# Other filler quotas in the attention stage, and GpSimd's long operations in pieces of 256 columns

## The chip, the cores and the metric

The kernel runs on one NeuronCore of a Trainium2 chip. The metric is the device time of one execution in microseconds (us), smaller is better. The engines are named as in the profile: PE is TensorE (matrix products and transposes), PEld its loads of weights, DVE is VectorE, ACT is ScalarE, POOL is GpSimd, SP is SyncE, which starts most of the transfers. Each engine works off its own instructions in a fixed order, and an instruction waits until what it needs from other engines is there.

## The reference, cut to what matters

One layer of a decoder for 1024 tokens of 1024 numbers. A normalized input goes through one projection into four token mixers (pooling, a short gated convolution, a Conformer convolution, differential attention with 4 heads), each 256 wide; their outputs go through one output projection and are added to the input; then comes a gated feed-forward part with 2816 inner columns.

```python
h = rms_norm(x, norm1_g)
z = h @ w_in                                   # 1024 x 2304, split into the mixers' inputs
# attention: two score maps per head, causal, with a bias per distance
p = softmax(sc, axis=-1);  a = p[:, :, 0] - lam * p[:, :, 1];  o = rms_norm(a @ v) * (1 - lam_init)
mix = concatenate([y_pool, y_sconv, y_conf, y_attn], axis=-1)
x = x + mix @ w_out
h2 = rms_norm(x, norm2_g)
x = x + (silu(h2 @ w_gate) * (h2 @ w_up)) @ w_down
```

All tensors are float32.

## The kernel before

**Products in three parts.** For TensorE each float32 matrix is split into a rounded part, hi, and the rest, lo = value - hi, and a product is the sum of three: hi times hi, hi times lo, lo times hi (`mm3`, L137 to L140; `mms`, L603 to L606, for the output projection). For a weight `wsplit` does this (L124 to L135): a transfer into the staging tile st, a cast to whi on the engine that a table names, and on GpSimd the subtraction to wlo, 128 x 1024, at L134.

**The attention stage** (some 220 to 450 us of the span). The tokens stand in four groups p of 256, and a unit is one p with one of four heads h: 16 units. For each half i of the group and each of the two score maps m, a unit makes scores on TensorE (sc, L673), VectorE adds the bias and takes the minimum (L680, L681), ScalarE makes the exponentials pt (L684), VectorE combines the two maps with a factor cf (L686 to L688). Then TensorE transposes pt (tp, L699), ScalarE and VectorE split it into at (L703, L704), and TensorE multiplies with the values (av, L708). After a second head the result oT is transposed (L720); after the fourth, VectorE normalizes the group. Ahead of the units the normalized queries qn are split and transposed (`stack_T`, L498 to L513): ScalarE makes the rounded part, GpSimd or VectorE the rest in kst (L506), TensorE transposes (L510). The two halves of a kst pair share one buffer: the second half can be written only when the transposes of the first are done.

**Fillers.** While a unit's chain runs, TensorE does other work in between: `gen_partial` (L608 to L635) is the output projection of the three other mixers in 16 items of 18 matmuls, 288 in all (tile fm, here called projections). For each item the mixer's tile is split into sp (lo on GpSimd, L627), the six weight tiles come from `load_wo`, and at the end ScalarE copies the sum and GpSimd adds the residual (x, L633, 14 of 16 items; the other two on VectorE). Later fillers are `out_attn` (L743 to L774, the attention's part of the output projection, its addition at L772), the second norm with its transposes (L190), and the first gate and up products of the feed-forward part (gu items). How many fillers follow each score, transpose and product is a list of numbers, FQ, one quota for each slot in order of time (`fill1`, L641); at the end of the attention stage the lists FA, FB and FC say it for the last groups. `tc.issue_after` keeps a filler behind the instruction to whose slot it belongs. When quotas are larger than what is left in the queue, nothing more is handed out.

**After it** come the products of the feed-forward part. `down0` (L1053 to L1068) does the first 256 rows of w_down: for each of two column halves a tile of 128 x 1024 is split into rhi (ScalarE) and rlo (GpSimd, L911), multiplied into pd, and VectorE adds pd to x (L1068). VectorE prepares differences of weights meanwhile (tb, L981).

Of the kernel before, what the change touches and what calls it, by code (L numbers as in the profile page):

```python
# [11 lines left out]
F = mybir.dt.float32  # L12
R = mybir.dt.float32r
AF = mybir.ActivationFunctionType
ALU = mybir.AluOpType
# [18 lines left out]
PQ0 = 2  # L34
PQ1 = 0
PO = [0, 1, 2, 3]
FQ = [13, 0, 1, 0, 4, 0, 0, 0, 0, 0, 5, 6, 1, 4, 0, 0, 0, 0, 6, 1, 2, 5, 1, 0, 3, 0, 0, 2, 0, 4, 0, 1, 6, 0, 1, 9, 0, 1, 0, 0, 3, 5, 0, 3, 1, 4, 0, 3, 2, 0, 0, 4, 0, 5, 2, 0, 1, 1, 0, 2, 0, 0, 0, 0, 1, 0, 2, 0, 0, 0, 7, 0, 0, 0, 0, 0, 0, 5, 5, 5, 5, 0, 2, 7, 2, 0, 0, 3, 3, 3, 3, 0, 1, 2, 0, 2, 2, 0, 0, 1, 1, 10, 0, 3, 1, 0, 3, 4, 0, 1, 0, 0, 12, 4, 2, 1, 3, 2, 8, 1, 3, 0, 2, 6, 2, 0, 1, 5, 4, 2, 2, 3, 2, 1, 2, 0, 1, 0, 0, 2, 1, 0, 0, 4, 0, 0, 1, 0, 3, 0, 1, 4, 0, 0, 0, 2, 0, 14, 6, 0, 1, 12, 2, 1, 9, 3, 0, 0, 0, 3, 1, 2, 13, 10, 0, 3, 0, 4, 0, 20]
FL = [9, 1, 2, 0, 0, 2]
N2F = 0
FA = [0, 5, 19, 17]  # L40
FB = [11, 1, 0, 0, 0, 0, 0, 0, 0, 0, 0, 0, 0, 0, 1, 0, 0, 0, 0, 0, 0, 0, 0, 0, 0]
FC = [11, 5, 5, 2]
X1 = [1, 1, 1, 1, 1, 1, 1, 1, 0, 1, 1, 1, 0, 1, 1, 1]
SPE = [2, 2, 1, 0, 0, 1, 0, 1, 1, 0, 0, 0, 0, 1, 2, 2, 0, 2, 0, 2, 0, 0, 0, 0, 0, 1, 0, 0, 0, 0, 0, 0, 1, 0, 0, 0, 2, 1, 0, 1, 2, 2, 2, 2, 2, 2, 0, 0]
WOE = [0, 0, 1, 0, 1, 0, 0, 0]
# [21 lines left out]
def tile_hybrid(ctx, tc, x, norm1_g, w_in, pool_w, pool_scale, sconv_w, conf_w, conf_b, ln_g, ln_b,  # L67
# [3 lines left out]
    V, A, G, T = nc.vector, nc.scalar, nc.gpsimd, nc.tensor  # L71
# [11 lines left out]
    def pool(name, bufs=1, side="left", **kw):  # L83
        return tc.tile_pool(name=name, bufs=bufs, side=side, reuse_waits="tile", **kw)
# [33 lines left out]
    def cp(e, dst, src):  # L118
        if e == 0:
            A.copy(dst, src)  # L120
        else:
            (V, G)[e - 1].tensor_copy(dst, src)

    def wsplit(view, shape, wpool=None, tag="w", stage=None, nv=0, eng=0):  # L124
        st = stage or stp.tile([P, 1024], F, name="st", tag="st")
        sh = "p (a b) -> p a b"
        dma(out=st.rearrange(sh, a=shape[0]), in_=view)
        hi = (wpool or wp).tile([P, 1024], R, name="whi", tag=tag)
        lo = (wpool or wp).tile([P, 1024], R, name="wlo", tag=tag)
        cp(eng, hi, st)  # L130
        if nv:
            V.tensor_tensor(lo[:, :nv], st[:, :nv], hi[:, :nv].bitcast(F), op=ALU.subtract)
        if nv < 1024:
            G.tensor_tensor(lo[:, nv:], st[:, nv:], hi[:, nv:].bitcast(F), op=ALU.subtract)  # L134
        return hi.rearrange(sh, a=shape[0]), lo.rearrange(sh, a=shape[0])  # L135

    def mm3(ps, L, Rr, first, last, more=False):  # L137
# [433 lines left out]

    hstk.close()
    psA.close()
    xp = ctx.enter_context(pool("xp", side="right"))
    x1 = [xp.tile([P, D], F, name=f"x1_{t}") for t in range(NT)]
    awk = ExitStack()
# [31 lines left out]
    def gen_partial():  # L608
        items = [(c, t) for c in range(2) for t in range(NT)]

        def prep(c, t):
            if t == 0:
                for kg in range(3):
                    wo[c, kg] = load_wo(kg, c)
            xr = stp.tile([P, 512], F, name="xr", tag="st")
            dma(out=xr, in_=x[t * P:(t + 1) * P, c * 512:(c + 1) * 512])
            return xr

        for c, t in items:
            xr = prep(c, t)  # L620
            ps = ps_fm()
            sl = slice(c * 512, c * 512 + 512)
            for kg, mix in enumerate((mixA, mixB, mixC)):
                sp = spp.tile([P, 2, 2, P], R, name="sp", tag="sp")
                src = mix[:, :, t * P:(t + 1) * P]
                cp(SPE[(c * NT + t) * 3 + kg], sp[:, 0], src)
                G.tensor_tensor(sp[:, 1], src, sp[:, 0].bitcast(F), op=ALU.subtract)  # L627
                W = wo[c, kg]
                for k in range(2):
                    yield from mms(ps, (sp[:, 0, k], sp[:, 1, k]), (W[0][:, k], W[1][:, k]), kg + k == 0, kg == 2 and k == 1)  # L630
            if X1[c * NT + t]:
                A.copy(x1[t][:, sl], ps)
                G.tensor_tensor(x1[t][:, sl], x1[t][:, sl], xr, op=ALU.add)  # L633
            else:
                V.tensor_tensor(x1[t][:, sl], xr, ps, op=ALU.add)  # L635

# [105 lines left out]
    def out_attn(p, ps_o=None):  # L742
# [17 lines left out]
        for i in range(2):  # L760
            t = 2 * p + i
            for c in range(2):
                po = ps_o()
                W = wo[3][c]
                for k in range(2):
                    yield from mms(po, (mh[:, k, i * P:(i + 1) * P], ml[:, k, i * P:(i + 1) * P]), (W[0][:, k], W[1][:, k]),
                                   k == 0, k == 1)
                sl = slice(c * 512, (c + 1) * 512)
                if X1B[PO.index(p)]:
                    tm = stp.tile([P, 512], F, name="tm", tag="st")  # L770
                    A.copy(tm, po)
                    G.tensor_tensor(x1[t][:, sl], x1[t][:, sl], tm, op=ALU.add)  # L772
                else:
                    V.tensor_tensor(x1[t][:, sl], x1[t][:, sl], po, op=ALU.add)  # L774

# [279 lines left out]
    def down0():  # L1055
        for c in range(2):
# [1 line left out]
            st = stage()  # L1058
            dma(out=st.rearrange("p (j c) -> p j c", j=2), in_=w_down[0:2 * P, sl].rearrange("(j p) c -> p j c", p=P))
            W = ring()  # L1060
            hilo(*W, st, G)
            W = [t.rearrange("p (j c) -> p j c", j=2) for t in W]
            for t in range(NT):
                ps = psdn.tile([P, 512], F, name="pd", tag="pd")
# [121 lines left out]
```

## Time and profile before

| | us |
|---|---|
| timed runs | 1077.08, 1077.14, 1079.26 (median 1077.14) |
| the profiled execution, its own time | 1077.97 |
| its span (first to last instruction) | 1076.2 |
| PE busy | 1045.2 (97%), 5203 matmuls |
| PEld busy | 875.9 (81%) |
| DVE busy | 736.7 (68%) |
| ACT busy | 439.8 (41%) |
| POOL busy | 222.9 (21%), 202 instructions |

The shares are means over a program whose stages have different limits. In the profile's 40 slices of equal length GpSimd is at work in the first 16, up to about 430 us, and then almost not at all. The chain of work that ended last goes through PE for 81% of the span, DVE 8%, DMA 4%, ACT 3% and POOL 1%.

### The profile page before, as it was taken

The numbers are of one execution on the slowest core, as the hardware profiler recorded it, in microseconds if no ns is written. First come the engines' busy times: TensorE is split into PE (matmuls) and PEld (weight loads), VectorE is DVE, ScalarE is ACT, GpSimd is POOL, SyncE is SP. The second block draws the span as 40 slices with busy tenths as digits, with TensorE's granted clock in tenths as the row PEclk, the third lists the DMA queues.
The fourth block names the chain that finished last, engine by engine and source line by source line (L and its number), as shares of the span: only waits on it lengthen the run. The fifth ranks groups of instructions, "written<-read, shape, count | busy, mean of one in ns | idle before, by whom it ended". The sixth has DMA issues, their size and how long they took to land.

```text
span 1076.2 us, 13520 instructions
## 1 busy us (share of the span) xinstructions
PE 1045.2 (97%) x5203; PEld 875.9 (81%) x5203; DVE 736.7 (68%) x1127; ACT 439.8 (41%) x710; POOL 222.9 (21%) x202
## 2 busy tenths in 40 slices
PE   7999999998989989899999999999999999999998
PEld 6878879996778877787888888888888878888886
DVE  5599995648899966886676566567657656755541
ACT  5512124536786766432432333333233343433320
POOL 5137124665675643000000000000000000000000
PEclk8999999999999999999999999999999999999999
DMA  8131110111021130022353454445255286866721
GB/s 217 49 98 40 59 40 21 40 41 40 30 79 41 49 93 25 9 61 88 117 207 101 162 206 148 131 171 200 94 176 205 101 311 230 295 196 212 233 103 40
DMA packets 89664, 128.04 MB, mean 119 GB/s; under 512 B 17112, under 2 KB 57600, under 8 KB 87040
## 3 DMA queue, kind: packets, MB, share of 16 engines
q1 hardware_dynamic: 89600, 127.18, 35.9%
q8 instruction: 41, 0.67, 0.3%
q14 instruction: 23, 0.19, 0.1%
HBM read 94.13 MB, written 33.04 MB: 118 GB/s over the span
## 4 chain that ended last, share of the span: by engine, by line
PE 81%; DVE 8%; DMA 4%; ACT 3%; issue 1%; POOL 1%; SPq 1%; ACTq 0%; POOLq 0%; DVEq 0%
PE sb L139 11%; PE sb L138 11%; PE sb L140 11%; PE mm L139 6%; PE mm L140 6%; PE mm L138 6%; PE dx L140 3%; PE dx L139 3%; PE dx L138 3%; PE dy L138 3%; PE dy L140 3%; PE dy L139 3%; PE fm L604 1%; PE fm L606 1%; PE fm L605 1%
## 5 line engine op out<-in xcount | busy, mean ns | idle before, releaser
L139 PE MATMUL sb<-T,rhi 128*128 128x512 f32 x320 | 124.6, 389 | 0.0
L140 PE MATMUL sb<-T,rlo 128*128 128x512 f32 x320 | 124.5, 389 | 0.0
L138 PE MATMUL sb<-T,rhi 128*128 128x512 f32 x320 | 124.5, 389 | 0.0
L911 DVE TENSOR_TENSOR dq<-ds,dq 128x2048 fp32r<-128x2048 f32 x35 | 79.9, 2290 | 57.0 <-ACT dq L910 53.9
L910 ACT CAST dq<-ds 128x2048 fp32r<-128x2048 f32 x35 | 66.6, 1912 | 105.8 <-PE dy L140 34.5
L134 POOL TENSOR_TENSOR wlo<-st,whi 128x1024 fp32r<-128x1024 f32 (+2 forms) x30 | 73.9, 2468 | 109.7 <-ACT whi L120 98.5
L138 PE MATMUL mm<-hT,whi 128*128 128x512 f32 (+1 forms) x224 | 79.6, 367 | 2.6 <-ACT whi L120 2.0
L139 PE MATMUL mm<-hT,whi 128*128 128x512 f32 (+1 forms) x224 | 81.4, 367 | 0.6 <-DVE hT L200 0.5
L140 PE MATMUL mm<-hT,wlo 128*128 128x512 f32 (+1 forms) x224 | 80.6, 363 | 0.3 <-POOL wlo L134 0.3
L317 DVE SCALAR_TENSOR_TENSOR t<-u,cw,t 128x1023 f32<-128x1023 f32 (+28 forms) x58 | 71.4, 1266 | 0.7
L140 PEld LDWEIGHTS sb<-T,rlo 128*128 128x128 f32 x320 | 60.1, 188 | 12.5
L138 PEld LDWEIGHTS sb<-T,rhi 128*128 128x128 f32 x320 | 60.1, 188 | 12.5
L139 PEld LDWEIGHTS sb<-T,rhi 128*128 128x128 f32 x320 | 60.1, 188 | 12.4
L910 ACT CAST rhi<-st 128x1024 fp32r<-128x1024 f32 x28 | 29.5, 1054 | 98.4 <-PE sb L139 49.5
L139 PE MATMUL dx<-dq 128*128 128x512 f32 x160 | 62.5, 390 | 1.3 <-DVE dq L911 1.3
L140 PE MATMUL dx<-dq 128*128 128x512 f32 x160 | 62.3, 390 | 0.0
L138 PE MATMUL dx<-dq 128*128 128x512 f32 x160 | 61.3, 390 | 0.0
L684 ACT ACTIVATE pt<-sc,mx 128x128 f32<-128x128 f32 (+7 forms) x64 | 47.6, 747 | 18.2 <-DVE mx L681 18.1
L138 PE MATMUL mm<-whi,hT 128*128 128x256 f32 x192 | 55.0, 290 | 0.0
L139 PE MATMUL mm<-wlo,hT 128*128 128x256 f32 x192 | 54.7, 286 | 0.0
L140 PE MATMUL mm<-whi,hT 128*128 128x256 f32 x192 | 54.5, 285 | 0.0
L1031 DVE TENSOR_TENSOR tp<-tp,sb 128x512 f32<-128x512 f32 x30 | 20.5, 684 | 45.2 <-PE sb L140 45.2
(342 smaller groups left out, 2698.3 us busy)
## 6 DMA issues: line engine op xcount, KB each, us to landing
ds<-dL SPq DMA_DIRECT2D x35, 512.0 KB, 4.1
wd<-in_w_down_dram SPq DMA_DIRECT2D x10, 1024.0 KB, 5.2
dT<-wd SPq DMA_DIRECT2D x10, 1024.0 KB, 6.0
dL<-afs SPq DMA_DIRECT2D x10, 1024.0 KB, 3.9
ds<-dT SPq DMA_DIRECT2D x20, 512.0 KB, 6.0
st<-in_w_in_dram SPq DMA_DIRECT2D x18, 512.0 KB, 3.8
st<-in_w_gate_dram SPq DMA_DIRECT2D x15, 512.0 KB, 4.2
st<-in_w_up_dram SPq DMA_DIRECT2D x15, 512.0 KB, 3.7
```

Source lines behind the costliest of these rows:

```text
L134: G.tensor_tensor(lo[:, nv:], st[:, nv:], hi[:, nv:].bitcast(F), op=ALU.subtract)
L138: T.matmul(ps, lhsT=L[0], rhs=Rr[0], start=first, stop=False, skip_group_check=more)
L139: T.matmul(ps, lhsT=L[0], rhs=Rr[1], start=False, stop=False, skip_group_check=more)
L140: return T.matmul(ps, lhsT=L[1], rhs=Rr[0], start=False, stop=last, skip_group_check=more)
L317: V.scalar_tensor_tensor((z if s == 30 else acc)[:, s:], u[:, :S - s], w[:, 30 - s:31 - s], acc[:, s:], op0=ALU.mult, op1=ALU.add)
L604: yield lambda: T.matmul(ps, lhsT=L[0], rhs=Rr[0], start=first, stop=False)
L605: yield lambda: T.matmul(ps, lhsT=L[0], rhs=Rr[1], start=False, stop=False)
L606: yield lambda: T.matmul(ps, lhsT=L[1], rhs=Rr[0], start=False, stop=last)
L684: A.activation(pts[m][:, 0:w], sc[:, 0:w], AF.Exp, bias=mx, scale=-1.0, accum_out=lt[:, h, m, i:i + 1])
L910: A.copy(hi, src)
L911: (eng or V).tensor_tensor(lo, src, hi.bitcast(F), op=ALU.subtract)
L1031: V.tensor_tensor(s, s, ps, op=ALU.add)
```

## The change

**Quotas.** 28 of the 180 numbers of FQ are others; their sum is 387 in both. FA goes from 41 to 53 in sum, FC from 23 to 15.

**Pieces.** A new helper `gpair` issues an operation of GpSimd in pieces of GW columns. GW is 1024, so one piece, until the attention stage begins, and 256 from there on. It is used for the wlo of weights loaded from then on (twelve of 128 x 1024: six and two of w_out, four of the gate and up weights), for the additions to x in `gen_partial` (14 of 128 x 512) and `out_attn` (four of 128 x 512), and for down0's two rlo (128 x 1024).

```diff
-FQ = [13, 0, 1, 0, 4, 0, 0, 0, 0, 0, 5, 6, 1, 4, 0, 0, 0, 0, 6, 1, 2, 5, ...
+FQ = [16, 0, 1, 3, 4, 0, 0, 0, 3, 0, 7, 6, 1, 4, 0, 0, 0, 0, 6, 1, 2, 3, ...
...
-FA = [0, 5, 19, 17]
+FA = [0, 11, 19, 23]
...
-FC = [11, 5, 5, 2]
+FC = [6, 4, 3, 2]
...
+    GW = [1024]
+
+    def gpair(dst, a, b, op, n):
+        for c in range(0, n, GW[0]):
+            sl = slice(c, min(c + GW[0], n))
+            G.tensor_tensor(dst[:, sl], a[:, sl], b[:, sl], op=op)
...
         if nv < 1024:
-            G.tensor_tensor(lo[:, nv:], st[:, nv:], hi[:, nv:].bitcast(F), op=ALU.subtract)
+            gpair(lo[:, nv:], st[:, nv:], hi[:, nv:].bitcast(F), ALU.subtract, 1024 - nv)
...
     psA.close()
+    GW[0] = 256
...
                 A.copy(x1[t][:, sl], ps)
-                G.tensor_tensor(x1[t][:, sl], x1[t][:, sl], xr, op=ALU.add)
+                gpair(x1[t][:, sl], x1[t][:, sl], xr, ALU.add, 512)
...
                     A.copy(tm, po)
-                    G.tensor_tensor(x1[t][:, sl], x1[t][:, sl], tm, op=ALU.add)
+                    gpair(x1[t][:, sl], x1[t][:, sl], tm, ALU.add, 512)
...
-            hilo(*W, st, G)
+            A.copy(W[0], st)
+            gpair(W[1], st, W[0].bitcast(F), ALU.subtract, 1024)
```

What this does to the order of instructions is shown at three places. A row gives line, operation, tile written and tiles read, shape, and a count; the lines of the kernel after are up to nine higher.

GpSimd, from the first weight of w_out that is split beside the units to the first addition to x (wlo: a weight's rest; kst: a query half's rest; sp: a mixer tile's rest; x: the residual). Before:

```order
L134 TENSOR_TENSOR wlo<-st,whi 128x1024
L506 TENSOR_TENSOR kst<-qn_1380,kst 128x4x64
L134 TENSOR_TENSOR wlo<-st,whi 128x1024
L627 TENSOR_TENSOR sp<-mixB,sp 128x256
L627 TENSOR_TENSOR sp<-mixC,sp 128x256
L633 TENSOR_TENSOR x_0_2388<-x_0_2388,xr 128x512
```

After:

```order
L129 TENSOR_TENSOR wlo<-st,whi 128x256 x4
L513 TENSOR_TENSOR kst<-qn_1380,kst 128x4x64
L129 TENSOR_TENSOR wlo<-st,whi 128x256 x4
L635 TENSOR_TENSOR sp<-mixB,sp 128x256
L635 TENSOR_TENSOR sp<-mixC,sp 128x256
L129 TENSOR_TENSOR x_0_2388<-x_0_2388,xr 128x256 x2
```

The order is the same here, with four pieces or two in the place of one operation.

TensorE, the first kst pair of the attention stage, from the transposes of the first half to those of the second, which stand at 264.16 us in the trace of before (oT and pt: attention tiles; sc: scores; fm: projections). Before:

```order
L720 MATMUL tp<-ident,oT 128x128 x4
L510 MATMUL tp<-ident,kst 128x128 x4
L673 MATMUL sc<-KT_1365,QT 128x256 x2
L604 MATMUL fm<-whi,sp 128x512
L605 MATMUL fm<-wlo,sp 128x512
...
L673 MATMUL sc<-KT_1364,QT 128x384
L673 MATMUL sc<-KT_1365,QT 128x256
L510 MATMUL tp<-ident,kst 128x128 x4
```

After:

```order
L728 MATMUL tp<-ident,oT 128x128 x4
L517 MATMUL tp<-ident,kst 128x128 x4
L681 MATMUL sc<-KT_1365,QT 128x256 x2
L681 MATMUL sc<-KT_1364,QT 128x384
L681 MATMUL sc<-KT_1365,QT 128x256
L517 MATMUL tp<-ident,kst 128x128 x4
```

Seven projections between the two halves (two are shown) have gone to other places.

TensorE, the fourth kst pair, whose halves' transposes stand at 306.01 and 308.39 us in the trace of before. Before:

```order
L605 MATMUL fm<-wlo,sp 128x512
L606 MATMUL fm<-whi,sp 128x512
L720 MATMUL tp<-ident,oT 128x128 x4
L510 MATMUL tp<-ident,kst 128x128 x4
L673 MATMUL sc<-KT_1364,QT 128x512
L673 MATMUL sc<-KT_1364,QT 128x256
L673 MATMUL sc<-KT_1364,QT 128x512
L673 MATMUL sc<-KT_1364,QT 128x256
L510 MATMUL tp<-ident,kst 128x128 x4
```

After:

```order
L716 MATMUL av<-at,VV_1376 128x128
L681 MATMUL sc<-KT_1364,QT 128x512
L681 MATMUL sc<-KT_1364,QT 128x256
L728 MATMUL tp<-ident,oT 128x128 x4
L517 MATMUL tp<-ident,kst 128x128 x4
L614 MATMUL fm<-whi,sp 128x512
L681 MATMUL sc<-KT_1364,QT 128x512
L681 MATMUL sc<-KT_1364,QT 128x256
L612 MATMUL fm<-whi,sp 128x512
...
L517 MATMUL tp<-ident,kst 128x128 x4
```

Eighteen projections stand between the two halves where none stood, the eleven ahead of the oT transposes are gone, and two of the four scores stand ahead of the oT transposes.

## Rows read from the trace of the kernel before

**Rows 1.** Stretches: window, length, busy PE PEld DVE ACT POOL (count), clock, DMA, GB/s.

```profile
600.00:700.00 100.00, 100.00 (x443) 82.83 (x442) 65.17 (x89) 33.65 (x47) 0.00 (x0) 1.00 0.43 148
245.00:262.00 17.00, 14.16 (x71) 10.61 (x70) 14.62 (x55) 9.54 (x35) 9.31 (x10) 1.00 0.15 48
283.00:297.00 14.00, 12.41 (x72) 9.92 (x72) 12.30 (x41) 10.97 (x30) 8.10 (x11) 1.00 0.07 20
297.00:325.00 28.00, 24.35 (x146) 20.41 (x145) 27.32 (x67) 21.46 (x48) 20.50 (x17) 1.00 0.22 75
325.00:376.00 51.00, 51.00 (x292) 43.91 (x291) 47.43 (x105) 36.78 (x75) 31.02 (x36) 1.00 0.15 48
376.00:412.00 36.00, 32.32 (x176) 25.15 (x175) 26.66 (x48) 23.01 (x44) 17.15 (x13) 1.00 0.24 73
430.00:449.00 19.00, 16.21 (x75) 12.61 (x75) 15.97 (x38) 8.41 (x17) 0.89 (x2) 0.91 0.00 0
446.00:448.00 2.00, 2.00 (x6) 1.56 (x5) 2.00 (x6) 0.93 (x3) 0.00 (x0) 0.50 0.00 0
484.00:500.00 16.00, 14.38 (x63) 11.54 (x62) 12.77 (x17) 3.31 (x4) 2.38 (x1) 1.00 0.25 88
```

**Rows 2.** Timeline of TensorE: start, us, operation, tiles, shape, [idle before, releaser].

```profile
246.75 0.39 PE L673 MATMUL sc<-KT,QT 128*128 128x256 f32 x1 [0.78 <-ACT pt L684]
262.60 0.39 PE L605 MATMUL fm<-wlo,sp 128*128 128x512 f32 x1
262.83 0.39 PE L606 MATMUL fm<-whi,sp 128*128 128x512 f32 x1
264.16 0.66 PE L510 MATMUL tp<-ident,kst 128*128 128x128 f32 x4 [0.34 <-POOL kst L506]
292.05 0.66 PE L510 MATMUL tp<-ident,kst 128*128 128x128 f32 x4 [1.14 <-POOL kst L506]
306.01 0.60 PE L510 MATMUL tp<-ident,kst 128*128 128x128 f32 x4
308.39 0.66 PE L510 MATMUL tp<-ident,kst 128*128 128x128 f32 x4 [1.08 <-POOL kst L506]
314.01 0.74 PE L708 MATMUL av<-at,VV 128*128 128x256 f32 x4 [1.19 <-DVE at L704]
324.73 0.50 PE L605 MATMUL fm<-wlo,sp 128*128 128x512 f32 x1 [0.93 <-POOL wlo L134]
387.79 0.51 PE L708 MATMUL av<-at,VV 128*128 128x256 f32 x2 [1.27 <-DVE at L704]
443.40 1.55 PE L190 MATMUL tp<-ident,xn 128*128 128x128 f32 x8 [1.33 <-ACT xn L160]
491.05 0.51 PE L138 MATMUL pd<-rhi 128*128 128x512 f32 x1 [1.62 <-DVE x L1068]
```

**Rows 3.** Timeline of VectorE, single operations, columns as in Rows 2.

```profile
242.17 0.69 DVE L122 CAST whi<-st 128x1024 fp32r<-128x1024 f32 x1 [2.61 <-PE mm L139]
244.05 1.90 DVE L122 CAST whi<-st 128x1024 fp32r<-128x1024 f32 x1 [1.18 <-PE mm L139]
315.34 1.03 DVE L687 SCALAR_TENSOR_TENSOR cf<-lt,nlam,cf 128x1 f32<-128x1 f32 x1
487.79 2.60 DVE L981 TENSOR_TENSOR tb<-st,sc 128x512 f32<-128x512 f32 x1
```

**Rows 4.** Timeline of GpSimd, single operations, columns as in Rows 2.

```profile
243.00 2.40 POOL L134 TENSOR_TENSOR wlo<-st,whi 128x1024 fp32r<-128x1024 f32 x1 [11.13 <-PE mm L140]
262.69 0.73 POOL L627 TENSOR_TENSOR sp<-mixA,sp 128x256 fp32r<-128x256 f32 x1
263.38 0.72 POOL L506 TENSOR_TENSOR kst<-qn,kst 128x256 fp32r<-128x256 f32 x1
315.06 1.30 POOL L633 TENSOR_TENSOR x<-x,xr 128x512 f32<-128x512 f32 x1
487.46 2.38 POOL L911 TENSOR_TENSOR rlo<-st,rhi 128x1024 fp32r<-128x1024 f32 x1 [13.24 <-ACT rhi L910]
```

More of the change, by code (lines that the diff above doesn't have):

```diff
@@ L36 @@
 PO = [0, 1, 2, 3]
-FQ = [13, 0, 1, 0, 4, 0, 0, 0, 0, 0, 5, 6, 1, 4, 0, 0, 0, 0, 6, 1, 2, 5, 1, 0, 3, 0, 0, 2, 0, 4, 0, 1, 6, 0, 1, 9, 0, 1, 0, 0, 3, 5, 0, 3, 1, 4, 0, 3, 2, 0, 0, 4, 0, 5, 2, 0, 1, 1, 0, 2, 0, 0, 0, 0, 1, 0, 2, 0, 0, 0, 7, 0, 0, 0, 0, 0, 0, 5, 5, 5, 5, 0, 2, 7, 2, 0, 0, 3, 3, 3, 3, 0, 1, 2, 0, 2, 2, 0, 0, 1, 1, 10, 0, 3, 1, 0, 3, 4, 0, 1, 0, 0, 12, 4, 2, 1, 3, 2, 8, 1, 3, 0, 2, 6, 2, 0, 1, 5, 4, 2, 2, 3, 2, 1, 2, 0, 1, 0, 0, 2, 1, 0, 0, 4, 0, 0, 1, 0, 3, 0, 1, 4, 0, 0, 0, 2, 0, 14, 6, 0, 1, 12, 2, 1, 9, 3, 0, 0, 0, 3, 1, 2, 13, 10, 0, 3, 0, 4, 0, 20]
+FQ = [16, 0, 1, 3, 4, 0, 0, 0, 3, 0, 7, 6, 1, 4, 0, 0, 0, 0, 6, 1, 2, 3, 1, 0, 3, 0, 0, 3, 0, 4, 0, 1, 2, 0, 1, 5, 0, 1, 0, 0, 3, 3, 0, 3, 1, 4, 0, 3, 2, 0, 0, 4, 0, 10, 2, 0, 1, 1, 0, 2, 0, 0, 0, 0, 1, 0, 2, 0, 0, 0, 5, 0, 0, 0, 5, 0, 0, 5, 4, 4, 4, 0, 7, 3, 2, 1, 0, 2, 2, 2, 2, 0, 1, 2, 0, 2, 2, 0, 0, 1, 1, 7, 0, 3, 1, 0, 3, 4, 0, 1, 0, 0, 12, 4, 2, 1, 3, 2, 8, 1, 3, 0, 2, 6, 2, 0, 1, 5, 4, 2, 2, 3, 2, 1, 2, 0, 1, 0, 0, 2, 1, 0, 0, 4, 0, 0, 1, 0, 3, 0, 1, 4, 0, 0, 0, 2, 0, 14, 8, 0, 1, 12, 7, 1, 6, 2, 0, 0, 0, 3, 1, 2, 10, 10, 0, 3, 0, 4, 0, 20]
 FL = [9, 1, 2, 0, 0, 2]
 N2F = 0
-FA = [0, 5, 19, 17]
+FA = [0, 11, 19, 23]
 FB = [11, 1, 0, 0, 0, 0, 0, 0, 0, 0, 0, 0, 0, 0, 1, 0, 0, 0, 0, 0, 0, 0, 0, 0, 0]
-FC = [11, 5, 5, 2]
+FC = [6, 4, 3, 2]
 X1 = [1, 1, 1, 1, 1, 1, 1, 1, 0, 1, 1, 1, 0, 1, 1, 1]
```

## The prediction

> **What bounds the kernel now.** I read the page first: TensorE is busy for 97% of the span, so an edit that removes no TensorE work can only win back time in which TensorE stands idle. Then the table of stretches [rows 1]: from 600 to 700 us, late in the program, the engine is never idle, and in the stretches that the change touches it is idle for 2.84 us (245 to 262), 1.59 (283 to 297), 3.65 (297 to 325), nothing (325 to 376), 3.68 (376 to 412), 2.79 (430 to 449) and 1.62 us (484 to 500). That is 16.2 us, 1.5% of the span, and more than the whole of what can be won. The same rows show why it idles: VectorE is busy for 14.62 of 17 us and 27.32 of 28 us there, GpSimd for 20.50 of 28. Up to 325 us the attention units run as a chain score, VectorE minimum, ScalarE exponential, VectorE sum, transpose, and the fillers only plug the holes in it. Third, TensorE's single waits [rows 2] name the holes: the score at 246.75 waits for an exponential, the transposes at 308.39 (and, beside others, 292.05 and 264.16) for GpSimd's kst, 314.01 and 387.79 for VectorE's at, 324.73 for GpSimd's wlo, 491.05 for VectorE's x.
>
> **What stretches VectorE.** A cast of 1024 columns takes 0.69 us at 242.17 and 1.90 us at 244.05 [rows 3]. The long one ends 0.55 us after GpSimd's wlo of 243.00 (2.40 us) ends [rows 4], that is, it ran its 0.6 us after that and stood before. The cf of 315.34 has one column, takes 1.03 us and ends at 316.37, with the x addition that GpSimd began at 315.06 (1.30 us). The difference tb takes 2.60 us at 487.79, against down0's subtraction of 2.38 us from 487.46. So an operation of VectorE with only SBUF operands that meets one of GpSimd stands until that one has ended. In each of these, GpSimd's following operation did not lengthen the wait.
>
> **Part 1, the pieces.** GpSimd's cost has a fixed part: 256 columns begin 0.69 us after one another (262.69, 263.38), 512 take 1.30, 1024 take 2.40 [rows 4]. Four pieces take 4 x 0.69 + 0.03 = 2.79, 0.4 us more than one operation, two take 1.41, 0.1 more. Cut are 14 operations of 1024 (twelve weights, two in down0) and 18 of 512: 14 x 0.4 + 18 x 0.1 = 7.4 us more on GpSimd. It has 7.5 us free in 297 to 325 and more elsewhere [rows 1], so most is hidden; I charge 0.2 us and keep 1.5 as the bound, since GpSimd's order stands still at times in front of a kst. In return VectorE waits for the rest of a piece, at most 0.7 us, in place of the rest of 2.40 or 1.30. And the order shows two waits for GpSimd on each weight where one stood: the first half of wlo frees its matmuls after two pieces, 1.4 us, not after the whole.
>
> **Part 2, the quotas.** 28 of 180 entries change and their sum stays 387; the same matmuls are handed out, so the sum only moves holes. A projection costs 0.23 us (one begins at 262.60, the next at 262.83) [rows 2]. Place by place:
> - 245 to 262: the score at 246.75 stands behind the cast of 244.05; met by a piece of 0.7 us instead of the 2.40, it ends some 0.8 us sooner. Nine more projections stand ahead of the first av product, 2.0 us of work for the 2.84 us that are idle. Not all can be filled, as the same fillers push the chain. I take a gain of 1.3, between 0 and 2.3.
> - The first kst pair: seven projections and four scores stood between its halves, now four scores (the order of TensorE at the first pair). The idle time at 264.16 was 0.34 us with seven projections. At the pair of 306.01, which has no projection between, 2.4 us pass from half to half and TensorE idles for 1.08 of them [rows 2]; the first pair's scores are smaller, so that some 1.0 of such 2.4 us would be work. With x's pieces and another sp ahead of this kst in GpSimd's order, 1.3 to 2.4 us of idleness appear: a loss of 1.4, between 0.6 and 2.
> - 283 to 297: seven projections for five between the halves that end at 292.05 (1.14 idle): gain 0.6, between 0 and 1.2.
> - 297 to 325: eighteen projections, 4.1 us, now lie inside the pair of 306.01 (the order at the fourth pair) and cover its 1.08 us: gain 1.1. The eleven that leave the place before the oT transposes covered the copy of oT: loss 0.6. Four projections go between the av products that waited at 314.01 (1.19): 0.9, of which I give back 0.5, since the next av has lost its cover of six. The wlo wait at 324.73 (0.93) is halved by the half-weight: 0.5. The cf of 315.34 loses some 0.5 of its stretch, of which 0.3 reaches TensorE. Together 1.7, between -0.3 and 3.
> - 325 to 376: TensorE is full before; 0, or a loss up to 1.
> - 376 to 412: the wait of 1.27 at 387.79 ends with at, which stands in VectorE's order behind operations that can meet an x addition and a wlo. A piece of the addition ends up to 0.6 sooner than the whole (1.30 - 0.69), and from the wlo I take 0.2: 0.8 together, between 0 and 1.3.
> - 430 to 449: VectorE is the engine in use with TensorE (15.97 and 16.21 of 19). FA and FC look large, but the order moves only two matmuls ahead of norm2's first transposes, which VectorE waits for: loss 0.4. The idle time before 443.40 (1.33) was followed by a granted clock of 0.50 in 446 to 448, its lower level; if that does not recur, up to 1.7 comes back (0.09 x 19, from the mean clock of 0.91).
> - 484 to 500: tb meets a piece: 1.9 us of stretch becomes at most 0.7, and of the 1.62 idle at 491.05 I take 1.3, between 0 and 1.6.
>
> **Sum.** 1.3 - 1.4 + 0.6 + 1.7 + 0 + 0.8 - 0.4 + 1.3 - 0.2 = 3.7 us. The profiled execution took 1077.97 us, the median of the timed runs is 1077.14; I subtract from the median: 1073.4. With all bounds bad it is 5.3 us slower, with all good 10.5 faster; they will not all fall one way.
>
> **A rule on the clock.** The trace first: in 446 to 448 the clock is 0.50, its lower level of 1.2 GHz, after a wait of 1.33 us at 443.40; after 292.05, 314.01 and 491.05, waits as long, it stays 1.00 [rows 1, 2]. The Trainium skill, "TensorE: Matmul & The Clock Gate", section "What's actually happening", says that the throttled clock is the default and activity lifts it. By that rule the new hole at the first kst pair could bring the lower clock there (rival D, 1075.1); by the three waits it does not, and the sum stands. The three speak against, the one for it.
>
> **Rivals.**
> - A, VectorE's chain stays the bound up to 325 us, and moved fillers only move holes. For it: 27.32 of 28 us busy. The quotas then give nothing net there; what stays is 0.8 + 1.3 - 0.4 = 1.7, or 1075.4, no change that a measurement of this kernel (about 0.2%, 2.2 us) can tell. Chance 0.17.
> - B, the pieces act as one: back to back, they keep VectorE out until the last. Then the 0.8, 0.3, 0.8 and 1.3 of shorter waits go: gain 0.5, 1076.6. Against it: VectorE got in at the end of each operation met, with the next one queued. Chance 0.05.
> - C, slower: GpSimd becomes late for kst. Its order is fixed and now holds 7.4 us more, and VectorE's operations can push in at three more boundaries in each weight. There are six kst pairs; if each second half comes 1.2 us later than forecast, 7.2 us are lost against 3.7 won: 1080.6. It decides from 1 us per pair. For it: 20.50 of 28 us busy and three of the present waits. Chance 0.13.
> - D, the clock falls at the first pair as at 443.40. There 1.7 us were lost, and the same lost at the first pair gives 1075.1, at the edge of no change. Chance 0.04.
> - E, the clock stays up at 444 to 449: 1071.7. Chance 0.07.
>
> **How the numbers follow.** The forecast itself gets 0.54, E counts with it: faster 0.61. A, B and D are no change, 0.26. Slower 0.13. The range reaches from the forecast with three of its terms near their good ends (1068.5) to half of C (1079).
>
> **What will show it.** Right: the cast of 244.05 near 1.1 us, tb below 1.5, no idle time at the pair of 306.01, idle time of 1 to 2 us at the first pair, about 1 us less in 376 to 412, a wait at pd below 0.5. Wrong: idle time in 245 to 325 that adds up to 8 us as before, kst waits in new pairs, or VectorE's waits that last through several pieces.

## The result, and the profile after

The changed kernel takes 1096.24 us (median of four runs, 1093.52 to 1098.84), the kernel before 1077.29 in the same comparison: a ratio of 1.0176, interval [1.0159, 1.0192]. It is slower by 19 us; the prediction said 3.7 us faster, and its range ended at 1079. The four times stand in two pairs: two near 1093.6 with a mean granted clock of 0.995 and two near 1098.8 with 0.989. The profiled execution is of the second kind. The first pair has the mean clock of the profiled execution of before (0.995, 1077.97 us) and is 15.6 us slower than it, so most of the loss is there at an equal clock.

The page of the kernel after: span, and busy time with its share and the count of instructions.

```profile
span 1097.1 us, 13585 instructions
PE 1057.8 (96%) x5203; PEld 882.2 (80%) x5203; DVE 733.8 (67%) x1127; ACT 439.7 (40%) x710; POOL 233.4 (21%) x262
```

TensorE has the same 5203 matmuls and is busy for 12.6 us longer, which is no more work: more of it ran at the lower clock, and a matmul that stands alone shows longer than one in a row (0.50 us for 0.39). The other 8.3 us of the 20.9 by which the span grew are idle time. GpSimd is busy for 10.5 us longer, where the prediction reckoned with 7.4.

The stretches of the kernel after, in the columns of [rows 1]. The attention stage now ends some 21 us later, so the later rows no longer hold the same work.

```profile
245.00:262.00 17.00, 15.36 (x67) 11.13 (x66) 12.95 (x46) 8.10 (x30) 11.02 (x16) 0.90 0.16 48
297.00:325.00 28.00, 22.28 (x116) 16.88 (x115) 23.93 (x63) 19.88 (x48) 16.45 (x20) 0.97 0.10 29
325.00:376.00 51.00, 49.25 (x268) 40.98 (x267) 44.84 (x102) 33.30 (x72) 34.54 (x48) 0.98 0.18 58
376.00:412.00 36.00, 30.78 (x164) 24.76 (x163) 25.85 (x50) 21.35 (x41) 17.09 (x22) 0.91 0.17 51
484.00:500.00 16.00, 16.00 (x72) 13.25 (x71) 12.15 (x19) 6.70 (x9) 4.61 (x4) 1.00 0.11 33
```

The second row is the one to read: TensorE does 116 matmuls in 28 us where it did 146 in [rows 1], and VectorE, ScalarE and GpSimd are all less busy as well. No engine has become the bound; all wait more. In the third row the stretch that was full does 268 for 292. The clock column, 1.00 for these stretches in [rows 1], is lower in the first four rows. The stretches of the lower clock by themselves, the last of them outside the rows above:

```profile
251.00:255.00 4.00, 3.37 (x9) 2.47 (x10) 2.86 (x11) 2.94 (x11) 2.83 (x6) 0.59 0.23 66
323.00:327.00 4.00, 3.88 (x14) 3.05 (x14) 3.20 (x7) 3.12 (x8) 4.00 (x7) 0.57 0.09 10
398.00:406.00 8.00, 6.63 (x20) 5.35 (x21) 5.75 (x9) 5.05 (x10) 6.40 (x8) 0.57 0.00 0
466.00:470.00 4.00, 4.00 (x16) 3.30 (x16) 4.00 (x11) 1.79 (x5) 0.00 (x0) 0.60 0.00 0
```

Length times (1 - clock) gives 1.6 + 1.7 + 3.4 + 1.6 = 8.3 us of full speed lost, where the profiled execution of before had 1.7 (the last fall stands there too, at 446 in [rows 1]); the first 24 us of the program, where both have such stretches, are left out. So at most 6.6 us of this execution's loss is clock, less where TensorE would have waited anyway (it is idle for 1.4 us of the third row), and the rest is waits.

TensorE's long single waits in the kernel after, in the columns of [rows 2]:

```profile
268.60 0.89 PE L681 MATMUL sc<-KT,QT 128*128 128x384 f32 x2 [1.10 <-ACT pt L692]
269.92 0.66 PE L517 MATMUL tp<-ident,kst 128*128 128x128 f32 x4 [0.44 <-POOL kst L513]
...
306.12 0.61 PE L681 MATMUL sc<-KT,QT 128*128 128x512 f32 x2 [1.64 <-ACT pt L692]
...
322.32 0.66 PE L707 MATMUL tp<-ident,pt 128*128 128x128 f32 x4 [1.62 <-ACT QT L520]
...
390.98 0.67 PE L681 MATMUL sc<-KT,QT 128*128 128x512 f32 x2 [1.07 <-ACT pt L692]
...
399.37 0.80 PE L612 MATMUL fm<-whi,mh 128*128 128x512 f32 x1 [2.30 <-ACT mh L766]
...
465.01 0.55 PE L197 MATMUL tp<-ident,xn 128*128 128x128 f32 x2 [2.73 <-ACT xn L167]
```

Most of them end with ScalarE: a score waits until the exponential of an earlier score has freed its buffer. In the attention stage of before such a wait stands twice, with 0.78 us (246.75, [rows 2]) and 0.69 (251.02), 1.5 us together; in the kernel after it stands fifteen times, with 8.4 us.

Behind three of the seven rows stands one and the same thing in ScalarE's order. ScalarE in the kernel after, columns as before:

```profile
320.74 1.04 ACT L120 CAST whi<-st 128x1024 fp32r<-128x1024 f32 x1 [2.48 <-DMA st<-in_w_out_dram]
321.69 0.58 ACT L520 CAST QT<-tp 128x512 fp32r<-128x512 f32 x1
...
388.77 1.05 ACT L120 CAST whi<-st 128x1024 fp32r<-128x1024 f32 x1 [2.56 <-DMA st<-in_w_out_dram]
...
397.19 1.04 ACT L120 CAST whi<-st 128x1024 fp32r<-128x1024 f32 x1 [2.83 <-DMA st<-in_w_out_dram]
...
398.62 0.69 ACT L766 ACTIVATE mh<-tp,subg 128x512 fp32r<-128x512 f32 x1
```

The cast of a weight of w_out comes up in ScalarE's order 2.5 to 2.8 us before the weight has landed, ScalarE stands, and the copy to QT, the exponential or mh behind it comes late: TensorE's waits of 1.62 us at 322.32, 1.07 at 390.98 and 2.30 at 399.37 end with these, 5.0 us together. In the trace of before ScalarE waits for no weight between 245 and 376 us, and 0.34 us for one at 381.30.

How the loss grows is seen at landmarks that both kernels have: transposes on TensorE whose order among themselves is the same. The first row stands ahead of everything that the change touches. Its 1.2 us are there already at the 101st matmul of the program (25.19 us in before, 26.44 in after), where the two programs are the same, so they belong to the two executions; over the profiled executions of all kernels of this document this offset lies between -1.1 and 1.5 us against before. What the stage lost is the difference between two rows. "Fillers ahead" is how many fillers more the kernel after has done by then; each is work that it need not do later, so 0.23 us for each [rows 2] is taken off.

| transposes of | before | after | later | fillers ahead | lost so far |
|---|---|---|---|---|---|
| kst, ahead of the units | 237.58 | 238.82 | 1.24 | 0 | 1.2 |
| first oT | 260.56 | 266.22 | 5.66 | 18 | 1.5 |
| first kst pair, second half | 264.16 | 269.92 | 5.76 | 11 | 3.2 |
| second pair, second half | 275.52 | 282.87 | 7.35 | 6 | 6.0 |
| third pair, second half | 292.05 | 297.60 | 5.55 | 2 | 5.1 |
| fourth pair, second half | 308.39 | 318.74 | 10.35 | 6 | 9.0 |
| fifth oT | 325.97 | 337.99 | 12.02 | 0 | 12.0 |
| sixth pair, second half | 358.58 | 371.33 | 12.75 | 0 | 12.8 |
| seventh oT | 376.69 | 391.49 | 14.80 | 0 | 14.8 |
| eighth and last oT | 410.68 | 432.93 | 22.25 | 6 | 20.9 |
| norm2, as in 443.40 of [rows 2] | 443.40 | 465.01 | 21.61 | 0 | 21.6 |

The last product of down0 then begins 20.7 us later, so about 0.9 us come back behind the norm. Without the 1.2 us of the first row the stage itself costs 20.4 us up to the norm.

### The profile page after: what moved, and what is told of

The parts are those of the page before. It is cut to its first block, busy times and chain, and to the rows that moved or that the text cites. A ratio compares the mean times of both kernels' runs of the same rounds, so it can differ in the third digit from the quotient of the medians.

```text
span 1097.1 us, 13585 instructions
## 1 busy us (share of the span) xinstructions
PE 1057.8 (96%) x5203; PEld 882.2 (80%) x5203; DVE 733.8 (67%) x1127; ACT 439.7 (40%) x710; POOL 233.4 (21%) x262
## 4 chain that ended last, share of the span: by engine, by line
PE 57%; DMA 3%; DVE 2%; ACT 1%; issue 0%; SPq 0%; POOL 0%; ACTq 0%; DVEq 0%
PE sb L147 11%; PE sb L146 11%; PE sb L145 11%; PE dx L147 3%; PE dx L146 3%; PE dx L145 3%; PE dy L145 3%; PE dy L147 2%; PE dy L146 2%; DMA ds<-dT 1%; PE pd L146 1%; PE pd L145 1%; PE pd L147 1%; DMA ds<-in_w_down_dram 1%; DVE dq L919 1%; DMA dL<-afs 1%
## 5 line engine op out<-in xcount | busy, mean ns | idle before, releaser
L129 POOL TENSOR_TENSOR wlo<-st,whi 128x256 fp32r<-128x256 f32 (+2 forms) x66 | 80.0, 1240 | 115.1 <-ACT whi L120 104.3
L692 ACT ACTIVATE pt<-sc,mx 128x128 f32<-128x128 f32 (+7 forms) x64 | 47.3, 745 | 20.4 <-DVE mx L689 20.3
L120 ACT CAST whi<-st 128x1024 fp32r<-128x1024 f32 x28 | 29.3, 1050 | 57.4 <-PE mm L146 42.1
```

Of the source, the lines that this page charges most:

```text
L129: G.tensor_tensor(dst[:, sl], a[:, sl], b[:, sl], op=op)
L692: A.activation(pts[m][:, 0:w], sc[:, 0:w], AF.Exp, bias=mx, scale=-1.0, accum_out=lt[:, h, m, i:i + 1])
```

## The experiments

**Which half of the change.** Two kernels each leave one half away, two more take one group of quotas.

The new quotas without pieces:

```diff
-    GW[0] = 256
+    GW[0] = 1024
```

> The changed kernel with GpSimd's operations whole again (1024 and 512 columns), the new quotas kept. Theory 1, the quotas cost the time: the fillers now stand where TensorE delays the next score, and are missing where it waits; then this kernel is slow too, 1090 to 1100 us. Theory 2, the pieces cost it (rival C: GpSimd late for kst and sp): this one is as fast as the prediction's quotas without pieces, 1074 to 1079 us. Theory 3, only both together cost: 1077 to 1082 us.

Measured: 1099.09 us, ratio 1.0210 [1.0178, 1.0242]. All of the loss is there without a single piece.

The pieces with the old quotas (FQ, FA and FC of before in the changed kernel):

> The kernel before with the pieces of 256 columns alone, the old quotas kept. Theory 1 (quotas): within 3 us of before, 1074 to 1080 us, with tb and pd near 488 us shorter. Theory 2 (pieces): 1090 us or more. Theory 3 (both together): 1075 to 1080 us, so this run and the one with the quotas alone would both be near before.

Measured: 1075.19 us, ratio 0.9983 [0.9972, 0.9993]. The pieces alone make the kernel faster by some 2 us: the lowest time of all that ran, though not clear of the run with down0's pieces alone further below. So theory 1 holds, and rival C (GpSimd late for kst through the pieces) falls.

The early group of quotas alone, in the kernel before:

```diff
-FQ = [13, 0, 1, 0, 4, 0, 0, 0, 0, 0, 5, 6, ... 5, 1, 0, 3, 0, 0, 2, 0, 4, 0, 1, 6, 0, 1, 9, 0, 1, 0, 0, 3, 5, ...
+FQ = [16, 0, 1, 3, 4, 0, 0, 0, 3, 0, 7, 6, ... 3, 1, 0, 3, 0, 0, 3, 0, 4, 0, 1, 2, 0, 1, 5, 0, 1, 0, 0, 3, 3, ...
```

> The kernel before, whole operations, with the first 11 changed quotas of FQ alone (positions 0 to 41; they hand out 84 in both, so from there on the fillers stand as before). In the changed kernel the transposes of the first kst pairs up to 285 us came 7.4 us later than in before, with as many fillers done. Theory 1: 1082 to 1085 us, with that delay seen at the same place. If the pieces made that delay: 1076 to 1079 us.

Measured: 1098.39 us, ratio 1.0195 [1.0178, 1.0211]. The place was right, the size was not: nine numbers (not eleven, as the expectation counts) cost 21 us, some three to five times what the theory gave them, and as much as the whole change. The 7.4 us of the expectation were misread as well: of the 7.35 in the table 1.24 belong to the executions and six fillers are ahead, which leaves 4.7.

The middle group alone (fourteen quotas, positions 53 to 101):

> The kernel before, whole operations, with the twelve changed quotas of positions 53 to 101 alone (184 handed out in both by then). In the changed kernel some 5 us more were lost between the second and the fourth pair of heads (285 to 338 us). Theory 1: 1080 to 1083 us. If the pieces made it: 1075 to 1079 us, since these quotas cover the wait at the pair of 308 us.

Measured: 1088.91 us, ratio 1.0111 [1.0093, 1.0129]: again more than expected. Two groups make 32 us, while all quotas together make 22. The losses don't add up, so they can't be the sum of what each place loses. That was the new question.

**The small groups and a small dose.** The late group (positions 158 to 172) alone:

> The kernel before, whole operations, with the last five changed quotas of FQ alone (positions 158 to 172). Theory 1a, a changed quota costs what its own place loses (a hole where projections are gone, a delayed chain where they are added): the order moves few rows, so 1077 to 1081 us. Theory 1b, every change of the quotas throws the whole later order of scores, transposes and fillers out of step: only what follows 376 us is left for that, so 1077 to 1080 us; the two theories differ in the small early edit of this group.

Measured: 1082.32 us, ratio 1.0046 [1.0032, 1.0059], over what both theories said. In its trace the last oT transposes wait 1.27 us for VectorE's h2lo, a tile of the second norm: fillers of that norm stand ahead in VectorE's order.

FA and FC alone:

> The kernel before, whole operations and old FQ, with the new FA and FC alone. The prediction charged 0.4 us for them: 1077 to 1079 us. If they are part of the 16 us: 1080 us or more, lost between 430 and 450 us.

Measured: 1078.82 us, ratio 1.0017 [1.0007, 1.0026]: 1.6 us, between the two figures.

Three projections moved by some 10 us:

```diff
-FQ = [13, ... 0, 0, 6, 1, 2, ...
+FQ = [16, ... 0, 0, 3, 1, 2, ...
```

> The kernel before, whole operations, with three projections moved by some 10 us: 16 for 13 after the first score, 3 for 6 in the slot that stands ahead of the first oT transposes. All later quotas and the order of the rest of the attention stage stay as before. Theory 1a (own place): a fraction of the early group's loss, 0.5 to 2 us, 1078 to 1079.5 us. Theory 1b (whole later order): no change, 1076.5 to 1078 us, since the later order is unchanged; and the early group's loss is then mostly made past its last changed slot.

Measured: 1077.17 us, ratio 0.9999 [0.9990, 1.0008]. Nothing, as theory 1b said. In its profiled execution the landmarks come 0.5 to 1.0 us later from 288 us on, although the first of them is 0.3 us early, and the mean clock is 0.998 for 0.995, so a small loss of its own place may be covered by that.

The pieces in down0 alone:

> The kernel before with the pieces in down0's two rlo alone. The prediction's term for 484 to 500 us: 1.3 us gained, 1075.5 to 1077 us, tb at most 1.5 us and no wait over 0.5 us at pd. If the gain of the run with all pieces (2 us) came from the attention stage: 1077 to 1078 us.

Measured: 1075.74 us, ratio 0.9987 [0.9977, 0.9997]. Down0 gives 1.5 of the 2.0 to 2.2 us. Its tb after the change:

```profile
486.97 0.87 DVE L981 TENSOR_TENSOR tb<-st,sc 128x512 f32<-128x512 f32 x1
```

It takes 0.87 us where [rows 3] has 2.60, and no wait at pd is left but one of 0.26 us.

**The own place, or the later order.** The program's order on each engine is not written by the quotas alone. The scheduler builds it from its own estimate of what is ready when, and a filler that moves shifts what comes after. In the trace of the early group, TensorE's, VectorE's and ScalarE's orders are those of before again only from some 384 to 387 us on (in the time of before), although the quotas are equal from position 42 on. Some neighbours of the early group return much sooner: TensorE's order is that of before from 283 us on in the two halves below and from 298 to 300 us on in the others. (The expectations put this at the fifth unit, and the early group's order as another to the end of the stage; by the scores in the trace the return is in the seventh to ninth unit.) Such a pair tells the two causes apart.

The early group without its two smallest entries:

> The early group without its two smallest entries (positions 21 and 27 keep their old quotas, position 41 takes 2): the eleven projections that move forward in the first two units and the places that pay for them are the same, but the scheduler's order of all engines is that of before again from the fifth unit on, where the early group's stays another until the end of the attention stage. Theory A, the moved projections cost at their own places: nearly the early group's loss, 1092 to 1099 us. Theory B, most of it comes from the later order, which the scheduler builds anew from a small shift: only the 5 us that the early group had lost by 284 us remain, 1080 to 1085 us.

Measured: 1084.25 us, ratio 1.0065 [1.0043, 1.0086]. Theory B.

The group's two halves, each with the order returning. Eleven projections forward and paid back at once (positions 0, 3, 8, 10 against 11, 12, 13):

> Eleven projections moved forward inside the first two units (positions 0, 3, 8, 10), paid back at once (positions 11 to 13 hand out none). Theory A: the score chain starts 11 x 0.23 = 2.5 us later and that stays to the end, with the eleven missing at the products of the second unit: 1079 to 1083 us. Theory B allows the same here, since the later order is that of before: 1078 to 1082 us. A figure near before would say that the chain has that much slack.

Measured: 1080.28 us, ratio 1.0031 [1.0020, 1.0043]. The withdrawals alone:

> The withdrawals of the early group alone (positions 21, 32, 35 and 41 hand out fewer, 27 one more), with the eleven given at position 43 in place of ahead of them; the later order is that of before. Theory A: holes at the second kst pair and behind it as in the changed kernel (1.5 us and 0.7), 1078 to 1081 us. Theory B: the same or less. Above 1085 us both are wrong on the early group.

Measured: 1080.47 us, ratio 1.0032 [1.0022, 1.0042]. So 3.3 and 3.5 us for the halves where the later order stays, together 6.7, near the 7.2 of the kernel above, which moves nearly the same projections at once. Where the order stays, the two losses add up.

The main move of the middle group, with the order returning:

> Five projections moved from a transpose slot of the sixth unit (position 70, 7 to 2) to the third kst pair (position 53, 5 to 10), the main move of the middle group alone; the later order is that of before. The prediction forecast a gain of 0.6 us at this pair (its 1.14 us wait covered). Theory A: part of the middle group's 11 us, 1080 to 1083 us. Theory B: 1076 to 1079 us.

Measured: 1079.26 us, ratio 1.0029 [1.0015, 1.0043], 2.2 us of the middle group's 11.5; just past the upper end of what theory B gave, not a gain.

One projection then separates the cases. Against the early group, position 27 keeps 2 and position 41 takes 4:

```diff
-FQ = [16, ... 0, 0, 3, 0, 4, 0, 1, 2, 0, 1, 5, 0, 1, 0, 0, 3, 3, ...
+FQ = [16, ... 0, 0, 2, 0, 4, 0, 1, 2, 0, 1, 5, 0, 1, 0, 0, 3, 4, ...
```

> The early group with one projection fewer moved: position 27 keeps 2 and position 41 takes 4, all else as in the early group (1098.4 us). With that the order of all engines from the fifth unit on is that of before. Theory B (the later order makes most of the loss): near the kernel whose order also returns, 1082 to 1087 us, though one projection only stands elsewhere. Theory A (own places): 1096 to 1099 us.

Measured: 1084.08 us, ratio 1.0069 [1.0054, 1.0085], against 1098.39 for the early group: 14 us from one projection in another slot. Clock is not the main part of it: of the single runs, 1085.68 us here and 1097.17 there have a mean clock of 0.993 and 0.992, and are 11.5 us apart.

Against this one, position 21 takes 4 and position 41 takes 3:

> The same as the one before with one projection moved again (position 21 takes 4, position 41 takes 3): now the later order is neither that of before nor quite that of the early group. Theory B: slow again, 1090 to 1100 us, since the later quotas were chosen for the order of before and stand at other work in any other. Theory A: as the kernel with one projection moved, within 2 us. If only the early group's own later order is bad: 1082 to 1088 us.

Measured: 1096.20 us, ratio 1.0187 [1.0170, 1.0204]. It is as slow, but its order is no third one: by the traces it is the early group's on all four engines from some 274 us up to some 323 us (in the time of the early group), with small shifts between neighbours behind. So this run repeats the early group's order with another projection moved. The order does it, not the count of projections at a place; that any other order would be slow is not shown by it.

The traces show what the other order does. Orders on TensorE at the fourth kst pair, first with one projection moved, then the early group:

```
L720 MATMUL tp<-ident,oT 128x128 x4
L510 MATMUL tp<-ident,kst 128x128 x4
L673 MATMUL sc<-KT_1364,QT 128x512
L673 MATMUL sc<-KT_1364,QT 128x256
L673 MATMUL sc<-KT_1364,QT 128x512
L673 MATMUL sc<-KT_1364,QT 128x256
L510 MATMUL tp<-ident,kst 128x128 x4
```

```
L720 MATMUL tp<-ident,oT 128x128 x4
L510 MATMUL tp<-ident,kst 128x128 x4
L673 MATMUL sc<-KT_1364,QT 128x512
L673 MATMUL sc<-KT_1364,QT 128x256
L673 MATMUL sc<-KT_1364,QT 128x512
L673 MATMUL sc<-KT_1364,QT 128x256
L673 MATMUL sc<-KT_1364,QT 128x512
L673 MATMUL sc<-KT_1364,QT 128x256
L673 MATMUL sc<-KT_1365,QT 128x512
L673 MATMUL sc<-KT_1365,QT 128x256
L510 MATMUL tp<-ident,kst 128x128 x4
```

The first is the order of before. In the second, four more score matmuls (two scores) stand ahead of the second half. TensorE there with one projection moved, in the columns of [rows 2]:

```profile
310.53 0.60 PE L510 MATMUL tp<-ident,kst 128*128 128x128 f32 x4
310.89 0.94 PE L673 MATMUL sc<-KT,QT 128*128 128x512 f32 x4
312.92 0.66 PE L510 MATMUL tp<-ident,kst 128*128 128x128 f32 x4 [1.09 <-POOL kst L506]
```

And in the early group:

```profile
314.75 0.60 PE L510 MATMUL tp<-ident,kst 128*128 128x128 f32 x4
315.11 0.94 PE L673 MATMUL sc<-KT,QT 128*128 128x512 f32 x4
319.04 0.61 PE L673 MATMUL sc<-KT,QT 128*128 128x512 f32 x2 [2.99 <-ACT pt L684]
319.92 1.01 PE L673 MATMUL sc<-KT,QT 128*128 128x512 f32 x2 [0.27 <-ACT pt L684]
320.73 0.63 PE L510 MATMUL tp<-ident,kst 128*128 128x128 f32 x2
```

From half to half it is 2.39 us in the first and 5.98 in the second. The score at 319.04 has no buffer until an exponential has been taken from one, and TensorE, which works in order, stands with the projections behind it. ScalarE and then GpSimd of the early group in the same stretch, columns as before, show what else is late there:

```profile
315.85 1.04 ACT L120 CAST whi<-st 128x1024 fp32r<-128x1024 f32 x1 [1.64 <-DMA st<-in_w_out_dram]
316.80 0.58 ACT L513 CAST QT<-tp 128x512 fp32r<-128x512 f32 x1
317.27 0.41 ACT L505 CAST kst<-qn 128x256 fp32r<-128x256 f32 x1
...
318.11 0.78 ACT L684 ACTIVATE pt<-sc,mx 128x640 f32<-128x640 f32 x1
```

```profile
316.97 2.36 POOL L134 TENSOR_TENSOR wlo<-st,whi 128x1024 fp32r<-128x1024 f32 x1 [1.71 <-ACT whi L120]
319.28 0.74 POOL L506 TENSOR_TENSOR kst<-qn,kst 128x256 fp32r<-128x256 f32 x1
```

ScalarE stood for 1.64 us for a weight's transfer, with the copy to QT, kst and the exponentials behind it; GpSimd did that weight's wlo, and kst was ready at 320.02 only. With one projection moved the order is the other way round, on ScalarE and then on GpSimd:

```profile
311.17 0.59 ACT L513 CAST QT<-tp 128x512 fp32r<-128x512 f32 x1 [0.53 <-PE tp L510]
311.65 0.41 ACT L505 CAST kst<-qn 128x256 fp32r<-128x256 f32 x1
311.96 1.05 ACT L120 CAST whi<-st 128x1024 fp32r<-128x1024 f32 x1
```

```profile
312.14 0.73 POOL L506 TENSOR_TENSOR kst<-qn,kst 128x256 fp32r<-128x256 f32 x1 [1.79 <-ACT kst L505]
313.08 2.40 POOL L134 TENSOR_TENSOR wlo<-st,whi 128x1024 fp32r<-128x1024 f32 x1 [0.21 <-ACT whi L120]
```

The transfer is no slower in the early group: in both kernels it is issued 2.1 to 2.4 us before the transposes of the first half and takes 3.4 to 3.5 us from issue to landing. What differs is that the cast has come ahead of the copy to QT. So at this place the late scores and the late kst are one event: without the four score matmuls the transposes would have waited for kst nearly as long.

The same stands in all five kernels that lost 11 us or more. At the fourth kst pair the cast of w_out's weight stands directly ahead of a copy to QT in ScalarE's order and waits for its transfer: 1.64 us in the early group, 1.71 in the run that moves one projection once more, 2.48 in the changed kernel, 1.22 in the new quotas without pieces, 2.19 in the middle group. In before and in the kernels whose order has returned by then the cast stands behind such a copy and a kst cast, and it waits for nothing, or for 0.82 us in the main move of the middle group.

Summed up, from the second half of the third kst pair to the last oT transposes: 118.63 us in before (292.05 to 410.68), 122.55 with one projection moved (293.81 to 416.36), 135.66 in the early group (296.42 to 432.08). Rows of the clock column in the early group in that time:

```profile
306.00:309.00 3.00, 3.00 (x10) 2.34 (x9) 2.96 (x9) 2.93 (x7) 0.00 (x0) 0.53 0.02 5
320.00:323.00 3.00, 3.00 (x12) 2.81 (x13) 2.94 (x9) 1.18 (x3) 2.92 (x3) 0.50 0.52 175
392.00:395.00 3.00, 3.00 (x10) 2.45 (x10) 2.15 (x6) 2.51 (x5) 1.42 (x1) 0.51 0.13 29
405.00:408.00 3.00, 3.00 (x14) 2.71 (x13) 0.69 (x1) 1.07 (x2) 1.27 (x1) 0.53 0.00 0
```

Each of the four costs at most some 1.4 us in the 3 us shown, 1.7 with its ends: 6.8 in all. With one projection moved the clock was 1.00 all along. Of the 13.1 us by which the early group is longer than that kernel here, at most 6.8 are thus clock and at least 6.3 waits, in one execution of each.

## Why the prediction was wrong

**The step that failed** is the one ahead of part 2: "the same matmuls are handed out, so the sum only moves holes". It priced each place by itself, and took the stretches in between, whose quotas are unchanged, as they stood in the trace of before. The runs say otherwise. The early group's halves cost 3.3 and 3.5 us where the later order returns, and the whole costs 14 us more where it doesn't. In the new order casts of weights stand in front of the attention chain before their transfers have landed, a wait that the sum does not have. The order of the changed kernel was at hand, and the prediction shows two kst pairs of TensorE's order and the start of GpSimd's; it did not ask whether the order returned to that of before, nor what stood in front of waits on ScalarE.

**245 to 262**, forecast a gain of 1.3, brought a loss of 0.3 by the first oT (1.2 to 1.5 in the table). The clock falls there at 251 to 255, which takes up to 1.6. Where it stays at 1.00 (the early group, its neighbour with one projection moved, and the new quotas without pieces), the same quotas gain 0.8 by the first oT, reckoned as in the table. The term was right in direction and within its bounds, and the clock covered it.

**The first kst pair**, forecast a loss of 1.4, lost 1.7. This term was right in size and only in part in its mechanism: kst, which the forecast named, makes TensorE wait 0.44 us at 269.92, where 0.34 stood; the larger wait is that of the score at 268.60 for an exponential, 1.10 us.

**The second kst pair** was not priced, although four of its thirteen projections were gone, and up to its second half another 2.7 us were lost. The term was missing.

**283 to 297**, forecast a gain of 0.6: the loss falls from 6.0 to 5.1, a gain of 0.9. Right.

**297 to 325**, forecast a gain of 1.7, lost 6.9 (5.1 to 12.0 by the fifth oT). The wait at the pair of 306.01 is covered, as said; no wait for kst stands there in the kernel after, though a projection there waits 0.65 us at 314.75 for ScalarE's copy to x. But the score at 306.12 waits 1.64 us and the transposes at 322.32 wait 1.62 for QT, behind the cast that waits for its weight at 320.74: holes that the trace of before didn't have. The clock's fall at 323 to 327 takes up to 1.7 more. This is the largest wrong term.

**325 to 376**: forecast 0 with a loss up to 1; 2.8 were lost from the fifth oT to the seventh, 1.07 of it in the wait at 390.98 behind the cast of 388.77.

**376 to 412**, forecast a gain of 0.8, lost 6.1 (14.8 to 20.9): 2.30 is the wait that ends at 399.37, behind the cast of 397.19, and up to 3.4 the clock, which falls during that wait.

**430 to 449**: forecast a loss of 0.4, and 0.7 were lost up to the norm. Alone, FA and FC cost 1.6, four times the 0.4 of the forecast. Whether the clock's fall stays was open in the forecast: it stays here (466 to 470), and is gone in the run with the pieces alone, where another stands at 251 to 255 instead.

**484 to 500 and the pieces** were right. The forecast said tb below 1.5 us and the cast near 1.1. In the kernel after, on VectorE:

```profile
245.29 0.93 DVE L122 CAST whi<-st 128x1024 fp32r<-128x1024 f32 x1 [1.18 <-PE mm L146]
509.53 0.92 DVE L989 TENSOR_TENSOR tb<-st,sc 128x512 f32<-128x512 f32 x1
```

The gain taken for down0 was 1.3, measured 1.5 alone; all pieces together 2.0 to 2.2. Rival B (the pieces act as one) falls with these rows. What the pieces cost GpSimd was taken too low, 0.4 us for 1024 columns and 7.4 in all, where its busy time grew by 10.5. In the kernel after:

```profile
244.25 3.27 POOL L129 TENSOR_TENSOR wlo<-st,whi 128x256 fp32r<-128x256 f32 x4 [10.72 <-PE mm L147]
```

It is 0.87 us more than the 2.40 of [rows 4]. The mean over the eleven weights from 243 us on is 3.02 us for 2.53, 0.5 more, and down0's two took 4.61 and 3.27 for 2.39. That the pieces alone still gain agrees with the cover that the forecast named.

**The clock.** Rival D put one more fall at the first kst pair. None stands there, but three others do that before had not. The one at 251 to 255 cannot be laid to the new quotas: the middle group alone, whose TensorE order and waits are those of before up to 290 us (0.78, 0.80 and 0.69 us ahead of 251 for 0.78, 0.81 and 0.69), has a clock of 0.57 in these 4 us, and before has 1.00. The same wait can end either way: a score that waits 2.09 us behind an exponential is at 302.30 in the kernel without the two smallest entries and at 301.64 in the one with one projection moved, and the rows after it are these, in that order:

```profile
304.00:308.00 4.00, 4.00 (x14) 3.18 (x13) 3.48 (x10) 3.05 (x7) 1.06 (x1) 0.57 0.02 6
302.00:306.00 4.00, 3.84 (x21) 3.10 (x20) 4.00 (x11) 2.91 (x8) 0.42 (x1) 1.00 0.00 0
```

One falls to 1.2 GHz, the other stays at 2.4. The Trainium skill, "TensorE: Matmul & The Clock Gate", section "What's actually happening", has it that activity lifts the clock from a throttled default. That in before and after the falls come in the first 24 us and in the stage with holes, and none from 480 us on, agrees with it; these rows show that one hole does not decide it. The prediction gave the rule one place and 0.04; over a whole stage with more holes the clock took up to 6.6 us in the profiled execution, and the two pairs of times, 5 us apart at 0.995 and 0.989, are of that size.

**The rivals.** A, VectorE's chain as the bound up to 325 us, comes nearest, in that moved fillers move the holes with them. But it forecast that nothing is gained, not that much is lost, and VectorE, busy for 27.32 of the 28 us from 297 us on in before, is busy for 23.93 of them in the kernel after. The slower rival, C, had the wrong cause. A rival in which other quotas change the order of everything behind them was not on the list. The sum's bad bounds add up to 5.2 us and its good ones to 10.1, not 5.3 and 10.5; nothing hangs on that.

**What stays open.** The five slow kernels share one place where the order went wrong (the cast that waits for its weight at the fourth kst pair); that moving this cast alone would win the time back was not tried, and the waits at other places were not taken apart. The slow orders that ran are no proof that every other order is. Why the clock falls in one execution and not in another is open. And the late group's 5 us was not taken apart further.

## What to carry to other kernels

Where a scheduler orders the engines, compare the whole order before and after a change of counts or quotas first: as long as it returns to the old one, the loss or gain of a place can be read from that place, and here two such losses added up; where it doesn't return, every later stretch has to be read anew, since quotas that are unchanged now stand at other work. When an in-order engine gets more fillers ahead of a dependent chain, price the delay of the chain as well as the hole that is filled. Look in the new order for an operation that waits for a transfer and now stands ahead of the chain. And before landmarks of two traces are compared, take off the offset that they have ahead of the change. Test the halves of a combined change singly: here one of them was a gain of 2 us hidden behind a loss of 22.

## What the runs showed of the hardware

Moving one projection between two slots changed the time by 14 us, 1.3%; TensorE's clock was at most half of that in the profiled executions, and 11.5 us stood between two runs of nearly equal clock (0.993 and 0.992). With the same order and the same waits the clock fell to 0.57 over 251 to 255 us in one execution and stayed at 1.00 in another. An operation of VectorE that meets one of GpSimd waits for the running piece only: tb went from 2.60 us to 0.87 and 0.92 as rlo was issued in four pieces. The four pieces of a wlo took 0.5 us longer than the whole in the mean of eleven (3.02 for 2.53), and 0.87 longer than the 2.40 of [rows 4] in the one shown.
